# Matmuls that walk their columns from last to first: a two-layer encoder on one core of Trainium2

## The chip, the cores and the metric

The kernel runs on one core of one Trainium2 chip. The time of a run is the device time of that core in microseconds (us). Three runs of the kernel before stand at 1179.58, 1178.33 and 1178.8 us, so the median is 1178.8 us. One further execution was recorded by the hardware profiler; every row of a trace below comes from such a profiled execution.

A core has a matrix unit (TensorE, called PE), which multiplies a stationary tile that it holds by a moving tile that streams through it column by column, and writes the product into a bank of the accumulator memory PSUM. VectorE (DVE), ScalarE (ACT) and GpSimd (POOL) do elementwise work and reductions; SyncE (SP) issues most of the transfers. The loading of a stationary tile is shown on a row of its own, PEld.

## The reference, cut to what matters

The input is x of 512 tokens by 1024 channels in float32. Two layers follow one another. In each, x is normalised, scaled and shifted by a vector from the conditioning c, and projected by `w_in` (1024 by 7328 columns). The projection feeds three attention branches that run over the same 512 tokens: one with low-rank keys and values (MLA, 8 heads), one over a window of three blocks of 128 keys with a sink (SWA, 8 heads), and one that subtracts two softmaxes (differential, 4 heads). Each branch result is gated, projected back and merged:

```python
h = rms_norm(x, g_pre[l]) * (1.0 + scale) + shift
(cq, ckv, kr, za, qb_, kb_, vb_, zb, qc, kc, vc, zc, gcols) = split_cols(h @ w_in[l], IN_SPLITS)
o_a = (mla_branch(...) * jax.nn.silu(za)) @ w_o_mla[l]
o_b = (swa_branch(...) * jax.nn.silu(zb)) @ w_o_swa[l]
o_c = (diff_branch(...) * jax.nn.silu(zc)) @ w_o_diff[l]
g = jax.nn.sigmoid(gcols).reshape(B, S, N_BRANCH, D)
y = (g[:, :, 0] * o_a + g[:, :, 1] * o_b + g[:, :, 2] * o_c) @ w_out[l]
x = x + gate * rms_norm(y, g_post[l])
```

All of it is asked for in float32.

## The kernel before, in words

Almost every product is made of float32 values that are split in two parts, a rounded high part and what is left of it (dtype float32r in the code). A product of two split operands is three matmuls into the same bank: high by high, high by low, low by high. That is `mm3` (lines 86 to 89). It is called for the projections (`proj_T`, `mla_in_step`), the MLA weights, scores and values, the products with the attention weights of the differential branch, the merges (`merge_steps`) and the output projection (`out_phase`). Where one operand carries its two parts stacked in the partitions, two matmuls do: the scores of the SWA branch (lines 878 and 879), those of the differential branch (lines 952 and 953), and `av_step` (lines 713 to 717) for attention weights by values. Sums over the channels that are to be on all partitions are products with a tile of ones (lines 300 and 301 in `gate_rows`, 983 and 984 in `diff_attention`).

The moving tile is float32r, 512 columns wide in nearly all cases, 416 in the first projection of a layer and 256 or 384 in the SWA scores. The matmul's result covers the same number of columns of one bank. All tiles are walked in ascending column order: column 0 of the moving tile goes to column 0 of the bank first.

Other work on PE: transposes against an identity tile (lines 704, 823, 630, 631, 381, 346, 171; moving tile of 128 columns at most), and a few products with one column or in plain float32 (lines 194, 212, 257, 438).

The weights stream from HBM through `wunit`: SP issues a 512 KB load into a `wr` buffer, ACT makes the rounded high part (line 81), DVE subtracts it from the whole (line 84), and PE takes both as stationary tiles. ACT and DVE also empty the eight banks of PSUM: softmax, squares, copies into the split form. A bank is read after the last matmul of its group has ended, and it is used again after its readers have ended.

The order of the work on each engine is set by the framework's planner: `tile.TileContext(nc, schedule_with_timeline_sim=True)` (line 1216) orders instructions by its own estimates of durations and by the priorities that the kernel gives (`tc.high_priority`, `behind`). Dependencies between instructions, and so the semaphores they wait on, follow from the tiles that they read and write.

Of the kernel before, what the change touches and what calls it, by code (L numbers as in the profile page):

```python
# [50 lines left out]
def hybrid_kernel(ctx, tc, x, c, w_ada, b_ada, g_pre, g_post, w_in, g_q, w_uq, g_kv, w_ukv,  # L51
# [6 lines left out]
    pe, act, dve, pool, sp = nc.tensor, nc.scalar, nc.vector, nc.gpsimd, nc.sync  # L58
# [24 lines left out]
    def sub(out_, a, b, eng=None):  # L83
        return (eng or dve).tensor_tensor(out=out_, in0=a, in1=b, op=ALU.subtract)  # L84

    def mm3(o, ah, al, bh, bl, start, stop):
        pe.matmul(o, ah, bh, start=start, stop=False)  # L87
        pe.matmul(o, ah, bl, start=False, stop=False)  # L88
        pe.matmul(o, al, bh, start=False, stop=stop)  # L89

    fence = []

# [39 lines left out]
    onesr = T("onesr", [P, P], F32R)  # L132
# [151 lines left out]
    def gate_rows(l):  # L284
        bg_step(100)
        acc = gate_acc[0]
        gg = []
        for hf in range(2):
            lo = hf * S
            g = T("x5", [P, 896])  # L290
            sp.dma_start(out=g[:, :S], in_=b_ada[l:l + 1, 2 * D + lo:2 * D + lo + S]
                         .broadcast_to([P, S]))
            gp = T("tf", [P, S])
            sp.dma_start(out=gp, in_=g_post[l:l + 1, lo:lo + S].broadcast_to([P, S]))
            pg = Q("sc")
            ah = T("pt", [P, S], F32R)
            al = T("pt", [P, S], F32R)
            act_copy(ah, acc[:, lo:lo + S])
            sub(al, acc[:, lo:lo + S], f(ah))
            pe.matmul(pg, onesr, ah, start=True, stop=False)  # L300
            pe.matmul(pg, onesr, al, start=False, stop=True)
            dve.tensor_tensor(out=g[:, :S], in0=pg, in1=g[:, :S], op=ALU.add)
            dve.tensor_tensor(out=g[:, :S], in0=g[:, :S], in1=gp, op=ALU.mult)
            gg.append(g[:, :S])
        return gg
# [404 lines left out]

    def av_step(av, v, ph, pl, first, last):
        if not last:
            pe.matmul(av, v, ph, start=first, stop=False)  # L713
            pe.matmul(av[0:64], v[:, 0:64], pl, start=False, stop=False)  # L714
        else:
            pe.matmul(av[0:64], v[:, 0:64], pl, start=False, stop=False)
            pe.matmul(av, v, ph, start=False, stop=True)

    def mla_attention(l, cl, kp, v, wts):
        o_all = []  # L720
# [131 lines left out]
    def swa_attention(l, qs, kk, vt):  # L852
        o_all = []
        bt = []

        def first(idx):
            g, n = idx // NT, idx % NT
            kh, kl = kk[g]
            if n == 0:
                bt.clear()  # L860
                for i in range(2):
                    b = T("x5", [P, 896])
                    for h in range(2):
                        sp.dma_start(out=b[:, h * 384:(h + 1) * 384],
                                     in_=skewed(bias_s[4 * g + 2 * i + h], 511, 384))
                    bt.extend([b[:, 0:384], b[:, 384:768]])
                o_all.extend(T("o", [P, S]) for _ in range(2))
            k0, k1 = max(n - 1, 0), min(n + 2, NT)
            j0 = (k0 - n + 1) * P
            w = (k1 - k0) * P  # L870
            mx, sm, nm, sk, rr = (stat(4) for _ in range(5))
            pr = T("p", [P, NT, S])
            for i in range(4):
                q = qs[4 * g + i]
                s = Q("sc")
                ts_ = slice(n * P, (n + 1) * P)
                ks_ = slice(k0 * P, k1 * P)
                pe.matmul(s[:, :w], q[:, ts_], kh[:, ks_], start=True, stop=False)
                pe.matmul(s[:, :w], q[:, ts_], kl[:, ks_], start=False, stop=True)
                dve.tensor_tensor_reduce(  # L880
                    out=pr[:, i, :w], in0=s[:, :w], in1=bt[i][:, j0:j0 + w], scale=1.0,
                    scalar=sinkt[:, l * 8 + 4 * g + i:l * 8 + 4 * g + i + 1],
                    op0=ALU.add, op1=ALU.max, accum_out=mx[:, i:i + 1])
                dve.tensor_scalar(out=nm[:, i:i + 1], in0=mx[:, i:i + 1], scalar1=-1.0,  # L884
                                  scalar2=None, op0=ALU.mult)
                act.activation(out=pr[:, i, :w], in_=pr[:, i, :w], func=AF.Exp,  # L886
                               bias=nm[:, i:i + 1], accum_out=sm[:, i:i + 1])
            dve.tensor_tensor(out=sk, in0=sinkt[:, l * 8 + 4 * g:l * 8 + 4 * g + 4], in1=nm,
                              op=ALU.add)
            act.activation(out=sk, in_=sk, func=AF.Exp)  # L890
            dve.tensor_tensor(out=sk, in0=sk, in1=sm, op=ALU.add)
            dve.reciprocal(out=rr, in_=sk)  # L892
            for i in range(4):
                pool.tensor_scalar(out=pr[:, i, :w], in0=pr[:, i, :w], scalar1=rr[:, i:i + 1],  # L894
                                   scalar2=1.0, op0=ALU.mult, op1=ALU.mult)
            return pr

        def second(idx, pr):
            g, n = idx // NT, idx % NT
            ob = o_all[2 * g:2 * g + 2]  # L900
            k0, k1 = max(n - 1, 0), min(n + 2, NT)
            av = Q("av")
            for kb in range(k0, k1):
                ph, pl = transposed_block([pr[:, i, (kb - k0) * P:(kb - k0 + 1) * P]
                                           for i in range(4)])
                av_step(av, vt[:, kb * 2 + g], ph, pl, kb == k0, kb == k1 - 1)
            ol = T("ta", [P, S])
            act_copy(ol[0:64], av[64:128])
            for i in range(4):
                dve.tensor_tensor(out=ob[i // 2][(i % 2) * 64:(i % 2) * 64 + 64, n * P:(n + 1) * P],  # L910
                                  in0=av[0:64, i * P:(i + 1) * P],
                                  in1=ol[0:64, i * P:(i + 1) * P], op=ALU.add)

        pipelined(first, second, 2 * NT)
        return o_all

# [20 lines left out]
    def diff_attention(l, hh, hl, fill):  # L937
# [3 lines left out]
        def first(hd):  # L941
            qq, kh, kl, vt = ops[hd]
            b = T("x5", [P, 896])
            sp.dma_start(out=b, in_=skewed(bias_d[hd], 1023, 896))
            pr = T("p", [P, NT, S])
            for t in range(NT):
                ts_ = slice(t * P, (t + 1) * P)
                mx, nm, sm, rr = (stat(2) for _ in range(4))
                pc = [pr[:, t], T("ta", [P, S])]
                for i in range(2):  # L950
                    s = Q("sc")
                    pe.matmul(s, qq[i][:, ts_], kh[i], start=True, stop=False)  # L952
                    pe.matmul(s, qq[i][:, ts_], kl[i], start=False, stop=True)  # L953
                    dve.tensor_tensor_reduce(out=pc[i], in0=s, in1=b[:, 384 - t * P:896 - t * P],
                                             scale=1.0, scalar=-3.0e38, op0=ALU.add, op1=ALU.max,
                                             accum_out=mx[:, i:i + 1])
                    dve.tensor_scalar(out=nm[:, i:i + 1], in0=mx[:, i:i + 1], scalar1=-1.0,  # L957
                                      scalar2=None, op0=ALU.mult)
                    act.activation(out=pc[i], in_=pc[i], func=AF.Exp, bias=nm[:, i:i + 1],  # L959
                                   accum_out=sm[:, i:i + 1])  # L960
                dve.reciprocal(out=rr, in_=sm)
                dve.tensor_tensor(out=rr[:, 1:2], in0=rr[:, 1:2], in1=lam_neg[l], op=ALU.mult)
                pool.tensor_scalar(out=pc[1], in0=pc[1], scalar1=rr[:, 1:2], scalar2=1.0,  # L963
                                   op0=ALU.mult, op1=ALU.mult)
                dve.scalar_tensor_tensor(out=pc[0], in0=pc[0], scalar=rr[:, 0:1], in1=pc[1],
                                         op0=ALU.mult, op1=ALU.add)
            return pr

        def second(hd, pr):
            vt = ops[hd][3]  # L970
            av = Q("av")
            for kb in range(NT):
                ph, pl = transposed_block([pr[:, t, kb * P:(kb + 1) * P] for t in range(NT)])
# [3 lines left out]
            sqh = T("pt", [P, S], F32R)  # L977
            sql = T("pt", [P, S], F32R)
# [1 line left out]
            act_copy(sqh, sq)  # L980
            sub(sql, sq, f(sqh))
            sq_ps = Q("pj")
            pe.matmul(sq_ps, onesr, sqh, start=True, stop=False)
            pe.matmul(sq_ps, onesr, sql, start=False, stop=True)
            rs = T("ta", [P, S])
            act.activation(out=rs, in_=sq_ps, func=AF.Ln, scale=1.0 / P, bias=epsc)
            act.activation(out=rs, in_=rs, func=AF.Exp, scale=-0.5)
            o = T("o", [P, S])
# [231 lines left out]
```

## Time and profile before

| what | number |
|---|---|
| median of 3 runs | 1178.8 us (1178.33 to 1179.58) |
| the profiled execution's own time | 1178.78 us |
| its span, first to last instruction | 1176.7 us |
| what lies around the span | 2.1 us |
| PE busy, matmuls | 1146.0 us (97%), 5428 matmuls |
| DVE busy | 844.2 us (72%) |
| ACT busy | 631.5 us (54%) |
| mean granted TensorE clock | 0.993 of full speed |

A matmul's busy time in these tables runs from its start to its modelled end and overlaps the next one's, so it isn't what a matmul costs in a dense stream. That cost is the distance between the starts of two matmuls that follow each other without a wait, which is read from the timeline. "PEclk" or "granted clock" is the share of full speed that the clock gate let through. In a row by groups the columns are line, engine, operation, output and inputs (the moving tile first), shapes, count, then busy time, mean ns of one, and the idle time before them with what ended it.

### The profile page before, as it was taken

What the parts mean: (1) busy time and instruction counts of PE and PEld (TensorE: products, weight loads), DVE (VectorE), ACT (ScalarE), POOL (GpSimd) and SP (SyncE); (2) the same over time, 40 slices, a digit from 0 to 9 for tenths busy, and PEclk for the clock granted to TensorE, in tenths of its full rate; (3) what the DMA queues carried; (4) which work ended last, traced back from release to release, by engine and by line L of the source; (5) the groups of instructions that cost most, each with busy time, mean ns of one, the idle gap of its engine ahead of it and who ended that gap; (6) DMA issues with size and microseconds to landing.
All of it is one profiled execution on the core that took longest, in us unless ns stands there. A gap on an engine that the chain in (4) does not pass through costs nothing.

```text
span 1176.7 us, 15536 instructions
## 1 busy us (share of the span) xinstructions
PE 1146.0 (97%) x5428; PEld 946.0 (80%) x5428; DVE 844.2 (72%) x1754; ACT 631.5 (54%) x1250; POOL 181.3 (15%) x226
## 2 busy tenths in 40 slices
PE   5899999999999999999999999999999999999997
PEld 4768788878887888888888888888888888888886
DVE  7956686898866687876577567688786568786654
ACT  5355464655543457664357456565564346675432
POOL 4310212122210010101211011222121001100120
PEclk9899999999999999999999999999999999999999
DMA  9537532256355433433454432324533333334442
GB/s 340 190 92 217 186 106 76 72 145 186 108 141 164 110 81 87 117 107 126 143 184 135 114 108 75 86 52 123 157 97 92 95 95 96 88 99 115 136 159 92
DMA packets 169522, 146.86 MB, mean 125 GB/s; under 512 B 7679, under 2 KB 146999, under 8 KB 169444
## 3 DMA queue, kind: packets, MB, share of 16 engines
q1 hardware_dynamic: 166148, 140.08, 40.9%
q10 hardware_dynamic: 3168, 5.77, 1.3%
q8 instruction: 43, 0.70, 0.2%
q14 instruction: 35, 0.29, 0.1%
q0 software_dynamic: 128, 0.01, 0.0%
HBM read 135.83 MB, written 14.20 MB: 127 GB/s over the span
## 4 chain that ended last, share of the span: by engine, by line
PE 84%; DVE 6%; DMA 3%; issue 3%; ACT 1%; POOL 1%; SPq 0%; DVEq 0%; POOLq 0%; ACTq 0%
PE ps_dn L87 20%; PE ps_dn L89 20%; PE ps_dn L88 19%; PE ps_tr L704 5%; PE ps_sc L89 2%; PE ps_sc L87 2%; PE ps_sc L88 2%; PE ps_av L714 1%; PE ps_av L713 1%; PE ps_sc L952 1%; PE ps_sc L953 1%; DMA wr<-in_w_in 1%; DVE o L206 1%; PE ps_pj L87 1%; PE ps_pj L88 1%
## 5 line engine op out<-in xcount | busy, mean ns | idle before, releaser
L87 PE MATMUL ps_dn<-hTh,wh 128*128 128x512 f32 x840 | 331.8, 395 | 1.4 <-DVE zz L479 0.8
L89 PE MATMUL ps_dn<-hTh,wl 128*128 128x512 f32 x840 | 330.5, 393 | 0.4 <-DVE wl L84 0.4
L88 PE MATMUL ps_dn<-hTl,wh 128*128 128x512 f32 x840 | 330.1, 393 | 0.0
L84 DVE TENSOR_TENSOR wl<-wr,wh 128x1024 fp32r<-128x1024 f32 x141 | 178.9, 1269 | 98.5 <-ACT wh L81 97.5
L81 ACT ACTIVATE wh<-wr 128x1024 fp32r<-128x1024 f32 x141 | 149.1, 1058 | 162.7 <-PE ps_dn L88 111.2
L87 PEld LDWEIGHTS ps_dn<-hTh,wh 128*128 128x128 f32 x840 | 158.2, 188 | 33.2 <-PE ps_dn L89 1.0
L89 PEld LDWEIGHTS ps_dn<-hTh,wl 128*128 128x128 f32 x840 | 158.0, 188 | 33.3 <-DVE wl L84 0.9
L88 PEld LDWEIGHTS ps_dn<-hTl,wh 128*128 128x128 f32 x840 | 158.1, 188 | 31.7
L84 DVE TENSOR_TENSOR pt<-ps_tr,pt 128x512 fp32r<-128x512 f32 x136 | 92.2, 684 | 30.5 <-ACT pt L81 29.6
L81 ACT ACTIVATE pt<-ps_tr 128x512 fp32r<-128x512 f32 x136 | 78.8, 596 | 64.8 <-PE ps_tr L704 63.6
L775 POOL TENSOR_SCALAR p<-p,st 128x512 f32<-128x512 f32 x64 | 52.2, 834 | 279.3 <-DVE st L773 243.7
L704 PE MATMUL ps_tr<-ident,p 128*128 128x128 f32 x544 | 92.4, 273 | 0.9 <-POOL p L775 0.6
L704 PEld LDWEIGHTS ps_tr<-ident,p 128*128 128x128 f32 x544 | 69.5, 141 | 20.2 <-POOL p L775 1.8
L87 PE MATMUL ps_dn<-u,wh 128*128 128x512 f32 x192 | 75.9, 395 | 0.0
L89 PE MATMUL ps_dn<-u,wl 128*128 128x512 f32 x192 | 75.9, 395 | 0.0
L88 PE MATMUL ps_dn<-u,wh 128*128 128x512 f32 x192 | 75.2, 391 | 0.0
L963 POOL TENSOR_SCALAR ta<-ta,st 128x512 f32<-128x512 f32 x32 | 26.7, 834 | 306.9 <-ACT wh L81 143.1
L894 POOL TENSOR_SCALAR p<-p,st 128x256 f32<-128x256 f32 (+1 forms) x64 | 42.1, 676 | 157.7 <-DVE st L892 130.4
L771 ACT ACTIVATE p<-ps_sc,st 128x512 f32<-128x512 f32 x64 | 43.7, 685 | 28.0 <-DVE st L770 27.7
L770 DVE TENSOR_REDUCE st<-ps_sc 128x1 f32<-128x512 f32 x64 | 43.4, 686 | 21.3 <-PE ps_sc L89 20.8
L886 ACT ACTIVATE p<-p,st 128x256 f32<-128x256 f32 (+1 forms) x64 | 35.7, 558 | 21.9 <-DVE st L884 21.2
L959 ACT ACTIVATE p<-p,st 128x512 f32<-128x512 f32 x32 | 23.1, 723 | 38.8 <-DVE st L957 38.7
(345 smaller groups left out, 2100.5 us busy)
## 6 DMA issues: line engine op xcount, KB each, us to landing
wr<-in_w_in SPq DMA_DIRECT2D x105, 512.0 KB, 3.7
wr<-in_w_ada SPq DMA_DIRECT2D x32, 512.0 KB, 3.6
wr<-in_w_out SPq DMA_DIRECT2D x16, 512.0 KB, 3.6
big<-in_w_ada SPq DMA_DIRECT2D x10, 512.0 KB, 7.6
big<-in_x SPq DMA_DIRECT2D x8, 512.0 KB, 5.3
wr<-in_w_o_mla SPq DMA_DIRECT2D x8, 512.0 KB, 4.0
wr<-in_w_o_swa SPq DMA_DIRECT2D x8, 512.0 KB, 3.4
wr<-in_w_o_diff SPq DMA_DIRECT2D x8, 512.0 KB, 3.7
```

The costliest lines, as they stand in the source:

```text
L81: return act.activation(out=out_, in_=in_, func=AF.Copy, scale=scale)
L84: return (eng or dve).tensor_tensor(out=out_, in0=a, in1=b, op=ALU.subtract)
L87: pe.matmul(o, ah, bh, start=start, stop=False)
L88: pe.matmul(o, ah, bl, start=False, stop=False)
L89: pe.matmul(o, al, bh, start=False, stop=stop)
L704: pe.transpose(tr[:, i * P:(i + 1) * P], b, ident)
L770: dve.tensor_reduce(out=nm[:, t:t + 1], in_=s, axis=AX.X, op=ALU.max, negate=True)
L771: act.activation(out=pr[:, t], in_=s, func=AF.Exp, bias=nm[:, t:t + 1], accum_out=sm[:, t:t + 1])
L775: pool.tensor_scalar(out=pr[:, t], in0=pr[:, t], scalar1=rr[:, t:t + 1], scalar2=1.0, op0=ALU.mult, op1=ALU.mult)
L886: act.activation(out=pr[:, i, :w], in_=pr[:, i, :w], func=AF.Exp, bias=nm[:, i:i + 1], accum_out=sm[:, i:i + 1])
L894: pool.tensor_scalar(out=pr[:, i, :w], in0=pr[:, i, :w], scalar1=rr[:, i:i + 1], scalar2=1.0, op0=ALU.mult, op1=ALU.mult)
L963: pool.tensor_scalar(out=pc[1], in0=pc[1], scalar1=rr[:, 1:2], scalar2=1.0, op0=ALU.mult, op1=ALU.mult)
```

## The change

A new helper, `rmm`, gives a matmul its output and its moving tile through views with the column axis reversed. The stationary tile is passed as it was. The last column of the moving tile is then read first, and its product is written to the last column of the bank first; each column of the bank still receives the product of the same column of the moving tile. `mm3` calls `rmm` three times, and the pairs of matmuls in `gate_rows`, `av_step`, `swa_attention` and `diff_attention` call it too. The transposes, the matmuls of lines 194, 212, 257 and 438, and all work on the other engines are as before.

```diff
+    def rmm(o, a, b, start, stop):
+        pe.matmul(o[:, ::-1], a, b[:, ::-1], start=start, stop=stop)
+
     def mm3(o, ah, al, bh, bl, start, stop):
-        pe.matmul(o, ah, bh, start=start, stop=False)
-        pe.matmul(o, ah, bl, start=False, stop=False)
-        pe.matmul(o, al, bh, start=False, stop=stop)
+        rmm(o, ah, bh, start, False)
+        rmm(o, ah, bl, False, False)
+        rmm(o, al, bh, False, stop)
...
-            pe.matmul(pg, onesr, ah, start=True, stop=False)
-            pe.matmul(pg, onesr, al, start=False, stop=True)
+            rmm(pg, onesr, ah, start=True, stop=False)
+            rmm(pg, onesr, al, start=False, stop=True)
...
     def av_step(av, v, ph, pl, first, last):
         if not last:
-            pe.matmul(av, v, ph, start=first, stop=False)
-            pe.matmul(av[0:64], v[:, 0:64], pl, start=False, stop=False)
+            rmm(av, v, ph, start=first, stop=False)
+            rmm(av[0:64], v[:, 0:64], pl, start=False, stop=False)
         else:
-            pe.matmul(av[0:64], v[:, 0:64], pl, start=False, stop=False)
-            pe.matmul(av, v, ph, start=False, stop=True)
+            rmm(av[0:64], v[:, 0:64], pl, start=False, stop=False)
+            rmm(av, v, ph, start=False, stop=True)
...
-                pe.matmul(s[:, :w], q[:, ts_], kh[:, ks_], start=True, stop=False)
-                pe.matmul(s[:, :w], q[:, ts_], kl[:, ks_], start=False, stop=True)
+                rmm(s[:, :w], q[:, ts_], kh[:, ks_], start=True, stop=False)
+                rmm(s[:, :w], q[:, ts_], kl[:, ks_], start=False, stop=True)
...
-                    pe.matmul(s, qq[i][:, ts_], kh[i], start=True, stop=False)
-                    pe.matmul(s, qq[i][:, ts_], kl[i], start=False, stop=True)
+                    rmm(s, qq[i][:, ts_], kh[i], start=True, stop=False)
+                    rmm(s, qq[i][:, ts_], kl[i], start=False, stop=True)
...
-            pe.matmul(sq_ps, onesr, sqh, start=True, stop=False)
-            pe.matmul(sq_ps, onesr, sql, start=False, stop=True)
+            rmm(sq_ps, onesr, sqh, start=True, stop=False)
+            rmm(sq_ps, onesr, sql, start=False, stop=True)
```

## The prediction, made before the changed kernel was built or run

> **What bounds the kernel now.** I read the page's busy table and clock line first, then the chain that ended last, then busy time by stretches, and last the timeline of PE. The first fence is from the page: the span, two engine rows, the granted clock in 40 slices, and the chain by engine and by line.
>
> ```profile
> span 1176.7 us, 15536 instructions
> PE 1146.0 (97%) x5428; PEld 946.0 (80%) x5428; DVE 844.2 (72%) x1754; ACT 631.5 (54%) x1250; POOL 181.3 (15%) x226
> ...
> PEclk9899999999999999999999999999999999999999
> ...
> PE 84%; DVE 6%; DMA 3%; issue 3%; ACT 1%; POOL 1%; SPq 0%; DVEq 0%; POOLq 0%; ACTq 0%
> PE ps_dn L87 20%; PE ps_dn L89 20%; PE ps_dn L88 19%; PE ps_tr L704 5%; PE ps_sc L89 2%; PE ps_sc L87 2%; PE ps_sc L88 2%; PE ps_av L714 1%; PE ps_av L713 1%; PE ps_sc L952 1%; PE ps_sc L953 1%; DMA wr<-in_w_in 1%; DVE o L206 1%; PE ps_pj L87 1%; PE ps_pj L88 1%
> ```
>
> The reader is to see that the chain is PE for 84% of the span, and within it the three lines of `mm3`. The next fence splits the span in three; its columns are the stretch, its length, then busy time and count of PE, PEld, DVE, ACT and POOL, the granted clock, the share of DMA and GB/s.
>
> ```profile
> 0.00:60.00 60.00, 41.10 (x196) 35.98 (x197) 49.40 (x122) 28.61 (x55) 24.21 (x29) 0.91 0.77 262
> 60.00:1150.00 1090.00, 1084.22 (x5144) 893.22 (x5143) 782.31 (x1608) 598.14 (x1181) 154.86 (x194) 1.00 0.41 118
> 1150.00:1176.70 26.70, 20.66 (x92) 16.77 (x90) 12.45 (x25) 4.71 (x16) 2.21 (x4) 0.96 0.21 79
> ```
>
> Between 60 and 1150 us PE lacks 1090.00 - 1084.22 = 5.8 us of being busy throughout, at full clock. So in 93% of the span a matmul that took longer would lengthen the kernel by just that much, and one that took less would shorten it, until DVE (782.31 us busy there) became the bound. Nothing covers a change in the cost of a matmul.
>
> What a matmul costs stands in the timeline: start in us, busy us, then the instruction. The first pair of rows is the first and the last of 15 matmuls of 512 columns in an unbroken stream; the second pair, the first and the last of four of 256 columns, with the transpose that follows them.
>
> ```profile
> 599.82 0.39 PE L87 MATMUL ps_dn<-big,op 128*128 128x512 f32 x1
> ...
> 602.99 0.40 PE L89 MATMUL ps_dn<-wh,pt 128*128 128x512 f32 x1
> ...
> 299.88 0.28 PE L878 MATMUL ps_sc<-op,op 128*128 128x256 f32 x1
> ...
> 300.23 0.28 PE L879 MATMUL ps_sc<-op,op 128*128 128x256 f32 x1
> 300.35 0.27 PE L704 MATMUL ps_tr<-ident,p 128*128 128x128 f32 x1
> ```
>
> From 599.82 to 602.99 are 14 distances, so 3.17 / 14 = 0.2264 us for 512 columns; from 299.88 to 300.35 are 4, so 0.118 us for 256. The difference is 0.109 us for 256 columns, 0.42 ns a column. The cost of a matmul is thus mainly its columns, with some 0.01 us that don't depend on them.
>
> **The change part by part.** Nothing is removed, added or moved among the instructions. Each call of `rmm` issues the one matmul that stood there, with the same stationary tile, the same number of columns, the same bank and the same flags. No transfer, no wait and no queue is touched, so nothing new stands behind a waiting instruction. What changes is the direction in which 4,664 matmuls step through the moving tile in SBUF and through the bank in PSUM. The count: the next fence has `mm3`'s three lines (stretches of the whole span restricted to lines 87, 88 and 89, in this order), and the groups of the paired matmuls.
>
> ```profile
> 0.00:1176.70 1176.70, 544.59 (x1392) 263.37 (x1392) 0.99 0.42 125
> ...
> 0.00:1176.70 1176.70, 544.67 (x1392) 262.85 (x1392) 0.99 0.42 125
> ...
> 0.00:1176.70 1176.70, 539.42 (x1392) 262.43 (x1392) 0.99 0.42 125
> ...
> L713 PE MATMUL ps_av<-pt,big 128*128 128x512 f32 x72 | 29.2, 406 | 0.9 <-DVE st L884 0.9
> ...
> L952 PE MATMUL ps_sc<-op,op 128*128 128x512 f32 x64 | 25.4, 407 | 0.0
> ...
> L717 PE MATMUL ps_av<-pt,big 128*128 128x512 f32 x32 | 12.6, 393 | 0.0
> ...
> L878 PE MATMUL ps_sc<-op,op 128*128 128x384 f32 x32 | 11.5, 360 | 0.0
> ...
> L878 PE MATMUL ps_sc<-op,op 128*128 128x256 f32 x32 | 8.9, 293 | 1.1 <-DVE st L880 1.1
> ...
> L983 PE MATMUL ps_pj<-pt,onesr 128*128 128x512 f32 x8 | 3.5, 434 | 0.0
> ...
> L300 PE MATMUL ps_sc<-pt,onesr 128*128 128x512 f32 x4 | 1.6, 389 | 0.0
> ```
>
> Three times 1,392 is 4,176. Each of the seven other groups has a partner of the same count in the line beside it (two matmuls a pair): 2 x (72 + 64 + 32 + 32 + 32 + 8 + 4) = 488. Together 4,664 of PE's 5,428; the other 764 are the transposes and small products. In columns: 64 matmuls have 384, 64 have 256, and 192 of `mm3`'s have 416 (8 channel blocks x 4 token blocks x 3 matmuls x 2 layers, from `mla_in_step`); the other 4,344 have 512. That makes 2,344,960 columns, as many as 4,580 matmuls of 512 have.
>
> No row of this trace shows an operand of a matmul that is stepped through backwards, so the price of a column in that order is bounded from both sides. *From below:* a column can't go through faster than the clock, so at most the part that isn't columns could shrink. That part follows from a stretch where the clock was halved. The first row of the next fence is that stretch (its eighth number is the granted clock, 0.50); the other two are the first and the last of four matmuls of 512 columns in it.
>
> ```profile
> 36.00:37.50 1.50, 1.50 (x5) 1.13 (x4) 1.50 (x7) 1.00 (x2) 0.00 (x0) 0.50 0.92 280
> ...
> 36.08 0.63 PE L87 MATMUL ps_dn<-hTh,pt 128*128 128x512 f32 x1
> ...
> 37.36 0.63 PE L88 MATMUL ps_tr<-hTl,pt 128*128 128x512 f32 x1
> ```
>
> 1.28 us / 3 = 0.4267 us for 512 columns at half clock. If that is columns alone, they take 0.2133 us at full clock, and 0.2264 - 0.2133 = 0.013 us a matmul is the rest. If all of it went, 4,664 x 0.013 = 61 us would be gained: 1118 us is the floor. *From above:* the nearest row in which columns pass more slowly is the same one, at one column in two full-clock periods, 0.4267 us for 512, worked out below as a rival.
>
> Between these ends I take zero, an unchanged 0.2264 us. The row it leans on is the stream itself: each column is four bytes next to the one before it, in the moving tile and in the bank, and this neighbourhood is the same in either direction. All groups have even widths, so two neighbours that are fetched or written together going up are also together going down. A group of accumulating matmuls is reversed as a whole; column n of one matmul meets column n of the next 0.2264 us later, as before. Loading the stationary tile isn't touched, and its cover stays: a load takes 188 ns against 226 ns from matmul to matmul (first row below).
>
> ```profile
> L87 PEld LDWEIGHTS ps_dn<-hTh,wh 128*128 128x128 f32 x840 | 158.2, 188 | 33.2 <-PE ps_dn L89 1.0 <-DVE zz L479 1.0
> ...
> 307.55 0.48 PE L87 MATMUL ps_dn<-hTh,wh 128*128 128x512 f32 x1
> 307.87 0.39 PE L88 MATMUL ps_dn<-hTl,wh 128*128 128x512 f32 x1
> ```
>
> The sum: the profiled execution's span of 1176.7 us, plus 4,664 x 0, plus the 2.1 us around it, is 1178.8 us. The median of the three runs is 1178.8 too, so nothing has to be moved between them. For scale: 0.2% of the time, about what a measurement of this kernel can tell from no change, is 2.4 us, or 0.5 ns a matmul. A very small cost would be seen.
>
> **The rivals.**
>
> *Half rate (slower).* The full rate needs two neighbouring columns taken in one access, and the logic that pairs them only knows the upward step; going down, each column is an access of its own. The place is every one of the 4,664 matmuls, and it decides from the first, as nothing covers them. Price: 0.4267 - 0.2264 = 0.200 us for 512 columns by the half-clock row; 4,580 x 0.200 = 917 us, so 2096 us. If the 0.013 us stays on top, 4,580 x 0.213 = 977 us, so 2156 us. For it: 0.2133 of 0.2264 us are columns at the full clock, so a slower access has no slack to hide in, and the trace has no stepped operand that shows one. Against it: pairs stay neighbours in reverse.
>
> The Trainium skill speaks for this rival: "Advanced Engine Details and Errata", section "PSUM Cachelines", and "PSUM — Partial Sum Buffer", section "Specifications (TRN2)", say that PSUM has 8-byte lines and that any non-contiguous pattern slows matmuls significantly. By a strict reading a step of -1 is such a pattern, and the sum would be that of this rival. The first page adds that every two consecutive elements should be contiguous, which a backward walk over even widths fulfils; by that reading the sum is mine. No run so far shows either.
>
> *A small price for each matmul (slower).* The direction costs a turn at the start of each matmul, not a rate: the walk begins at the far end. Bounds: above zero, up to what a restart costs in this trace. The two rows just shown, right after a transpose, lie 0.32 us apart in place of 0.2264, so 0.09 us; for all 4,664 that is 420 us. A doubling of the 0.013 us is nearer to what is in question and gives 1178.8 + 61 = 1240 us. Against it: no first column of a stream has such a turn today.
>
> *Another order (either sign).* The planner orders the instructions by its own estimates. If it prices a reversed operand otherwise, the same instructions come in another order, and PE's few waits move. What can be lost or won is of the size of the gaps: 5.8 us between 60 and 1150 us, and those of the first 60 us, of which these are PE's waits on other engines:
>
> ```profile
> PE ps_sc L346 <- DVE st L318: 4.1, 1, 4.1
> PE ps_sc L87 <- ACT hTh L81: 2.9, 1, 2.9
> PE ps_tr L212 <- DVE o L206: 2.4, 1, 2.4
> ```
>
> So 1173 to 1185 us. For it: the priorities lie close together. Against it: shapes and types are the same.
>
> *A gain.* Some of the 0.013 us between matmuls goes: 1118 us at most, 1160 us for a third of it. I see nothing in the profile for it.
>
> *The change doesn't do what it says.* Both views are reversed, so the builder could turn both back and emit the old instructions. The time would be 1178.8 us, as in the forecast.
>
> **How the numbers follow.** The forecast of no change gets 0.50, and the builder that turns it back 0.02 with the same time. Half rate gets 0.24, because its only witness against is symmetry; the small price 0.10; another order 0.10, of which 0.04 faster, 0.02 within and 0.04 slower; a gain 0.04. So faster by over 0.2% is 0.08, within 0.2% is 0.54, slower is 0.38. The predicted time is the likeliest's, 1178.8 us; its own range is 1176 to 1182 us. That holds little over half, and with the small price still under 0.8, so the range has to reach into half rate, whose two ends are 2096 and 2156: it goes up to 2160 us. Downward it takes in the planner's gain and the smallest part of the other: 1170 us.
>
> **What would show it.** Right: the dense stream still has 0.226 us from start to start for 512 columns, `mm3`'s lines have 1,392 matmuls each with the same mean, 15,536 instructions, and the span is 1176.7 us. Half rate: the distance becomes 0.43 us at a granted clock of 1.00 while transposes keep theirs; the small price: 256 and 512 columns grow by the same ns; another order: distances unchanged, but the waits of PE and the sequence of lines differ. Wrong is the forecast if the distance for 512 columns moves by more than 0.5 ns, whichever way.

## The result: 1.6% slower, and the profile after

The changed kernel took 1197.91 us (median of 4 runs, 1197.23 to 1199.2) against 1179.19 us for the kernel before. The ratio is 1.0161, with a 95% interval of 1.0143 to 1.0178. The forecast was no change. The profiled execution of the changed kernel took 1197.91 us with a span of 1196.0 us.

The page of the changed kernel, the lines that answer to those shown of before. All reversed matmuls now stand on line 87, the line of `rmm`:

```profile
span 1196.0 us, 15542 instructions
PE 1168.5 (98%) x5428; PEld 947.7 (79%) x5428; DVE 846.4 (71%) x1754; ACT 631.8 (53%) x1250; POOL 180.4 (15%) x226
...
PEclk9899999999999999999999999999999999999999
...
PE 88%; DVE 5%; DMA 3%; issue 1%; ACT 1%; POOL 1%; SPq 0%; DVEq 0%; POOLq 0%; ACTq 0%
...
L87 PE MATMUL ps_dn<-hTh,wh 128*128 128x512 f32 x840 | 337.5, 402 | 0.2
```

The counts are the same, 5,428 matmuls; so is the granted clock. The mean of one projection matmul went from 395 to 402 ns, and PE has a larger share of the chain. The stretches of the changed kernel, in the columns used before, with the middle one ending where as much is left as in the kernel before (26.7 us):

```profile
0.00:60.00 60.00, 41.10 (x189) 35.80 (x190) 49.27 (x122) 28.90 (x55) 24.43 (x29) 0.89 0.77 262
...
60.00:1169.30 1109.30, 1106.71 (x5154) 895.60 (x5153) 785.28 (x1608) 598.75 (x1183) 153.74 (x194) 1.00 0.40 116
1169.30:1196.00 26.70, 20.65 (x89) 16.31 (x87) 11.84 (x25) 4.12 (x14) 2.21 (x4) 0.96 0.21 79
```

With both ends cut at the same length, the loss falls on the middle: 1109.30 us in place of 1090.00, with nearly the same work on the other engines. It holds 5,154 matmuls in place of 5,144; the ten more are some 2 us of it (an estimate at 0.23 us each). PE lacks 2.6 us of being busy throughout there, and lacked 5.8 before; it isn't waiting, it is slower. The timeline of PE in a dense stream, first and last of 11 matmuls:

```profile
615.02 0.40 PE L87 MATMUL ps_dn<-wh,op 128*128 128x512 f32 x1
...
617.35 0.40 PE L87 MATMUL ps_dn<-wl,op 128*128 128x512 f32 x1
```

2.33 us over 10 distances are 0.233 us, where the kernel before had 0.2264. PE executes the same instructions in the same order in both kernels, so the distance from each matmul's start to the next one's can be compared pair by pair. Worked out from the starts of all 5,428:

```text
512 columns, by distance before   count   mean before   mean after   sum of differences
up to 229 ns                       3255     226.7 ns      233.4 ns       +21.7 us
230 to 249 ns                       851     232.9         233.7           +0.7
250 to 340 ns                       211     314.5         317.1           +0.6
over 340 ns (waits)                  26     610.4         508.2           -2.7
all other matmuls                  1084                                   -0.8
```

So 3,255 matmuls went from 226.7 to 233.4 ns, which is 6.7 ns. The 851 that were at 230 to 249 ns already paid nearly nothing: 233 ns is a level that is reached, not an amount that is added.

At half clock there is no price at all. The changed kernel has a stretch like the one that the prediction used (its eighth number is the granted clock); the other rows are the first and the last of four reversed matmuls of 512 columns in it:

```profile
35.40:37.20 1.80, 1.80 (x6) 1.36 (x5) 1.80 (x8) 0.92 (x2) 0.00 (x0) 0.50 0.95 299
...
35.45 0.63 PE L87 MATMUL ps_dn<-hTl,pt 128*128 128x512 f32 x1
...
36.73 0.63 PE L87 MATMUL ps_tr<-hTh,pt 128*128 128x512 f32 x1
```

1.28 us / 3 = 0.4267 us, exactly what the ascending ones took in the kernel before. Of the eleven reversed distances of 512 columns at half clock ten are 426 or 427 ns; the eleventh, at the start of a stream, is 572, as its like in the kernel before is. The 416-column ones take 346 or 347 ns there, so 96 columns are 80 ns, 512 are 427, and nothing is left over. So neither the 6.7 ns nor the 13 ns that the prediction called the rest is an amount on top of the columns: both show only at the full clock. That would fit something that goes on beside the columns and is the longer of the two at full clock, but this is argued, not shown.

### The profile page after: what moved, and what is told of

The parts are those of the page before. It is cut to its first block, busy times and chain, and to the rows that moved or that the text cites. A ratio compares the mean times of both kernels' runs of the same rounds, so it can differ in the third digit from the quotient of the medians.

```text
span 1196.0 us, 15542 instructions
## 1 busy us (share of the span) xinstructions
PE 1168.5 (98%) x5428; PEld 947.7 (79%) x5428; DVE 846.4 (71%) x1754; ACT 631.8 (53%) x1250; POOL 180.4 (15%) x226
## 4 chain that ended last, share of the span: by engine, by line
PE 88%; DVE 5%; DMA 3%; issue 1%; ACT 1%; POOL 1%; SPq 0%; DVEq 0%; POOLq 0%; ACTq 0%
PE ps_dn L87 60%; PE ps_sc L87 11%; PE ps_av L87 7%; PE ps_tr L707 5%; PE ps_pj L87 4%; DVE o L209 2%; DMA wr<-in_w_ada 1%; DMA wr<-in_w_in 1%; DVE wl L84 1%; DVE u L254 1%; DVE hTl L84 0%; DMA rk<-in_rope_k 0%; PE ps_pj L826 0%; POOL p L778 0%; DMA tf<-in_g_pre 0%
## 5 line engine op out<-in xcount | busy, mean ns | idle before, releaser
L87 PE MATMUL ps_dn<-hTh,wh 128*128 128x512 f32 x840 | 337.5, 402 | 0.2
L87 PE MATMUL ps_dn<-hTh,wl 128*128 128x512 f32 x840 | 336.3, 400 | 0.2 <-DVE wl L84 0.2
L87 PE MATMUL ps_dn<-hTl,wh 128*128 128x512 f32 x840 | 336.1, 400 | 0.0
L87 PE MATMUL ps_sc<-op,op 128*128 128x512 f32 (+2 forms) x448 | 126.8, 383 | 0.8 <-DVE st L883 0.8
L87 PE MATMUL ps_dn<-u,wh 128*128 128x512 f32 x384 | 124.4, 400 | 0.0
L87 PE MATMUL ps_av<-pt,big 128*128 128x512 f32 (+1 forms) x304 | 100.6, 406 | 0.9 <-DVE st L887 0.9
L87 PEld LDWEIGHTS ps_sc<-op,op 128*128 128x128 f32 x448 | 79.5, 189 | 16.6 <-DVE st L883 1.0
L87 PEld LDWEIGHTS ps_dn<-u,wh 128*128 128x128 f32 x384 | 71.5, 188 | 16.4
L966 POOL TENSOR_SCALAR ta<-ta,st 128x512 f32<-128x512 f32 x32 | 26.7, 836 | 314.1 <-DVE st L965 132.5
L87 PEld LDWEIGHTS ps_av<-pt,big 128*128 128x128 f32 (+1 forms) x304 | 50.7, 170 | 14.7 <-DVE st L887 1.2
```

Source lines behind the costliest of these rows:

```text
L87: pe.matmul(o[:, ::-1], a, b[:, ::-1], start=start, stop=stop)
```

## The experiments

**Reading alone, and writing alone.** The reversal has two halves. Each was taken back by itself.

```diff
-        pe.matmul(o[:, ::-1], a, b[:, ::-1], start=start, stop=stop)
+        pe.matmul(o, a, b[:, ::-1], start=start, stop=stop)        # reading alone
+        pe.matmul(o[:, ::-1], a, b, start=start, stop=stop)        # writing alone
```

> Only the moving tile is read from last to first; the bank is written ascending, so the columns of every product come out mirrored, and the output is not the reference's. Instructions, order and waits are those of the changed kernel. Theory R (the price of 5.4 ns per 512-column matmul lies in reading the moving tile downward): the dense stream goes at 233 ns as after, and the time is about 1198 us (ratio to before 1.016). Theory W (it lies in writing the bank downward): 227 ns and 1179 us (ratio 1.000). Theory B (either direction has a part): in between, 1185 to 1193 us.

> Only the bank is written from last to first; the moving tile is read ascending, so the columns come out mirrored, and the output is not the reference's. Theory R: 227 ns from start to start and 1179 us. Theory W: 233 ns and 1198 us. Theory B: in between, and the two prices of the two runs add up to about 19 us.

Reading alone: 1198.96 us, ratio 1.0156 (1.0140 to 1.0171). Writing alone: 1180.19 us, ratio 1.0000 (0.9989 to 1.0012). The timeline of PE, reading alone (first and last of 12), then writing alone (first and last of 9):

```profile
599.09 0.40 PE L87 MATMUL ps_dn<-wh,op 128*128 128x512 f32 x1
...
601.65 0.40 PE L87 MATMUL ps_dn<-wh,pt 128*128 128x512 f32 x1
```

```profile
596.75 0.39 PE L87 MATMUL ps_dn<-wh,op 128*128 128x512 f32 x1
...
598.56 0.39 PE L87 MATMUL ps_dn<-wh,pt 128*128 128x512 f32 x1
```

2.56 us over 11 distances are 0.233 us; 1.81 over 8 are 0.226. Theory R holds: the whole price lies in reading the moving tile downward. Writing a bank from its last column to its first costs nothing that these runs can tell. The strict reading of the Trainium skill's "PSUM — Partial Sum Buffer", section "Specifications (TRN2)", that any non-contiguous pattern slows matmuls significantly, does not extend to a step of -1 in the bank.

**Streams without the encoder.** Does the price go by the matmul, by the column, or by the pair of neighbours?

```diff
+    for k in range(N):
+        pe.matmul(banks[1], st(k), mv(k), **fl(k))
+    for k in range(N):
+        pe.matmul(banks[2][:, ::-1], st(k), mv(k)[:, ::-1], **fl(k))
...
+    for k in range(N):
+        pe.matmul(banks[7], st(k), mv(k)[:, ::-1] if k % 2 else mv(k), **fl(k))
```

> Not the encoder: streams of 40 accumulating matmuls, one line of the kernel for each stream, with nothing else at work at first; the output is not the reference's. Ascending 512 columns: 226.7 ns from start to start; both reversed: 233.3 ns. Reading alone and writing alone reversed: theory R 233.3 and 226.7, theory W the other way round. If the price is a turn for each matmul, 496, 416, 384, 320 and 256 columns pay the same 6.7 ns; if it goes with the columns, 416 pay 5.4, 384 pay 5.0 and 256 pay 3.3. Alternating directions: the mean of both, 230 ns, if each matmul pays for itself; 226.7 or 233.3 if it goes by the pair. Blocks of 16 columns taken downward with ascending columns inside: 226.7 if single steps cost, 233.3 if the far end as starting point costs. Tile shifted by 2 or 14 columns: same prices if alignment plays no part. With loads under way, the ascending stream should show some distances of 231 to 236 as the kernel before does, and the reversed one should stay at 233.

The timeline of PE; each row is one stream, with its start, so the start of the next row less its own, over its count, is the distance. In order: 512 columns ascending, both reversed, reading alone, writing alone; then ascending and reversed at 416, 384, 320, 256 and 496; then alternating directions; then ascending from 2 columns later.

```profile
17.92 9.23 PE L46 MATMUL ps_b<-m,w 128*128 128x512 f32 x40
26.99 9.50 PE L48 MATMUL ps_b<-m,w 128*128 128x512 f32 x40
36.33 9.50 PE L50 MATMUL ps_b<-m,w 128*128 128x512 f32 x40
45.66 9.25 PE L52 MATMUL ps_b<-m,w 128*128 128x512 f32 x40
54.74 7.63 PE L54 MATMUL ps_b<-m,w 128*128 128x416 f32 x40
62.21 7.80 PE L56 MATMUL ps_b<-m,w 128*128 128x416 f32 x40
69.85 7.10 PE L58 MATMUL ps_b<-m,w 128*128 128x384 f32 x40
76.79 7.27 PE L60 MATMUL ps_b<-m,w 128*128 128x384 f32 x40
83.89 6.03 PE L62 MATMUL ps_b<-m,w 128*128 128x320 f32 x40
89.76 6.03 PE L64 MATMUL ps_b<-m,w 128*128 128x320 f32 x40
95.62 4.96 PE L66 MATMUL ps_b<-m,w 128*128 128x256 f32 x40
100.42 4.90 PE L68 MATMUL ps_b<-m,w 128*128 128x256 f32 x40
105.16 8.97 PE L70 MATMUL ps_b<-m,w 128*128 128x496 f32 x40
113.97 9.23 PE L72 MATMUL ps_b<-m,w 128*128 128x496 f32 x40
123.03 9.36 PE L74 MATMUL ps_b<-m,w 128*128 128x512 f32 x40
132.23 9.51 PE L76 MATMUL ps_b<-m,w 128*128 128x512 f32 x40
141.58 9.59 PE L78 MATMUL ps_b<-m,w 128*128 128x512 f32 x40
```

From L46 on the distances are 0.227, 0.2335, 0.233 and 0.227 us: reading costs, writing doesn't, with nothing else at work. At 416 columns it is 0.187 against 0.191, at 384 0.1735 against 0.1775, at 320 0.147 against 0.1465, at 256 0.120 against 0.1185, at 496 0.220 against 0.2265. The price is neither a fixed turn nor a rate. It is about 6.6 ns at 512 and 496, about 4 ns at 416 and 384, and none at 320 and 256 (the ascending stream of 416 was at 0.188 in the next run, which leaves 3 ns there). Alternating directions give 0.230, the mean, so each matmul pays for itself.

Blocks of 16 columns taken downward with ascending columns inside them went at 0.233 us, so single downward steps aren't needed for the price. Two things were not foreseen. Ascending blocks with descending columns inside went at 0.2665 us. And the ascending tile that begins 2 columns later (L76) went at 0.234 us, as slowly as a reversed one. In this run the loads meant to run beside the last streams had all landed by then, so it says nothing on loads at work there. They ran during the first two streams of 512 shown above, at some 290 GB/s by the page, and these still kept 0.227 and 0.2335 us.

**Where the tile begins, and other engines at work.** If an ascending tile can be slow by its place, is the reversed one slow only because it begins at an odd place, its column 511?

```diff
+    for k in range(N):
+        pe.matmul(banks[3], st(k), mv(k, S, 2), **fl(k))
...
+    for k in range(N):
+        pe.matmul(banks[6][:, ::-1], st(k), mv(k, S, 1)[:, ::-1], **fl(k))
```

> Not the encoder: streams of 24 accumulating matmuls, each line of the kernel with another first column of the moving tile, ascending or both views reversed; the last four streams have VectorE or ScalarE at work beside them; the output is not the reference's. The streams before showed that an ascending tile that begins 2 columns later goes at 233.8 ns and one that begins 14 later at 230, against 226.7. Theory S (the price goes with the place of the first column that is read, not with the direction): the ascending distance depends on the shift with a period of 4, 8 or 16 columns and is 226.7 again at 16; a reversed tile that starts on the right column (shifted by 1, from column 512 on) goes at 226.7. Theory D (reading downward costs by itself): no shift of the reversed tile comes below 233. Widths 416 and 384 reversed and shifted by 1: theory S gives back 186.7 and 173.3, theory D keeps 191 and 178. Beside VectorE or ScalarE: if their traffic makes the distances of 231 to 236 in the kernel before, the ascending stream shows such distances and the reversed one stays at 233.3.

Ascending, shifts of 1, 2, 3, 4, 6, 8, 10, 12, 14, 15 and 16 columns gave distances of 236.7, 233.3, 228.9, 231.7, 233.3, 233.4, 233.4, 233.4, 230.0, 226.8 and 228.8 ns, against 226.7 unshifted (means without the first few matmuls of a stream, which differ). No period of 4, 8 or 16. Reversed, no shift came below 233.3 ns; shifted by 1, so that it begins at column 512, it was 235.6, and by 3, the slowest, 239.8. At 416 and 384 columns the reversed streams took 191.0 and 177.7 ns unshifted, 193.4 and 177.9 shifted by 1, 189.0 and 179.7 shifted by 8. Of this run's timeline, the reversed stream without a shift, the ones shifted by 1 and 2, and the row that follows; then, with VectorE beside them, an ascending and a reversed stream, and the row after:

```profile
81.51 5.77 PE L71 MATMUL ps_b<-m,w 128*128 128x512 f32 x24
87.11 5.82 PE L73 MATMUL ps_b<-m,w 128*128 128x512 f32 x24
92.77 5.84 PE L75 MATMUL ps_b<-m,w 128*128 128x512 f32 x24
98.45 5.92 PE L77 MATMUL ps_b<-m,w 128*128 128x512 f32 x24
...
195.94 11.09 PE L125 MATMUL ps_b<-m,w 128*128 128x512 f32 x48
206.87 11.37 PE L130 MATMUL ps_b<-m,w 128*128 128x512 f32 x48
218.07 11.06 PE L135 MATMUL ps_b<-m,w 128*128 128x512 f32 x48
```

Theory S falls, theory D holds in this: at 512 columns a downward walk stays at 233 ns or more wherever it begins, and at 416 and 384 it doesn't go back to the 186.7 and 173.3 ns that theory S gave.

The ascending stream beside VectorE has a mean of 0.228 us, but not because of VectorE. Its slow distances are the first ten, 224 to 236 ns; the next thirty, still beside the additions (the last ends at 205.1 us), are 226 or 227. The one beside ScalarE's copies begins with 238 and 232 ns and keeps 226 or 227 from the third on. What these streams show is that a stream takes some matmuls to settle behind another one. The kernel before shows the same. Take the matmuls of 512 columns with a stationary tile of 128, in the order in which they follow one another without a different matmul or a gap (250 ns or more) between them. Of the first ten in such a row, 741 of 1,426 took 230 ns or more; of the later ones, 39 of 2,598. Of the later ones with VectorE busy for over 95% of the distance it was 14 of 1,393, of those with under 5% 14 of 764. So most of the 851 slow ones stood near the start of a row, and nothing here puts them down to VectorE. Why a row settles so is open.

**The stationary tile.** The next stationary tile is loaded while the moving tile streams: PEld is busy for 947.7 us beside PE's 1168.5. Do the two reads clash?

```diff
+    for k in range(N):
+        pe.matmul(banks[1][0:16], st(k, 16), mv(k), **fl(k))
+    for k in range(N):
+        pe.matmul(banks[2][0:16][:, ::-1], st(k, 16), mv(k)[:, ::-1], **fl(k))
```

> Not the encoder: streams of 24 accumulating matmuls of 512 columns in pairs, ascending and then both views reversed, with stationary tiles of 128, 96, 64, 32 and 16 columns, stationary tiles that begin 1 to 64 columns later, one stationary tile for all, one moving tile for all, and both operands out of one tile; the output is not the reference's. Theory L (the price is a clash of the downward walk with the loading of the next stationary tile, which goes on meanwhile): price falls with the columns of the stationary tile, about 3.3 ns at 64 and 1 ns or nothing at 16, and the distance of the ascending stream falls too; it changes with the start of the stationary tile. Theory M (it lies in the walk over the moving tile alone): 6.7 ns at every size of the stationary tile and at every start of it.

Its timeline, the pair at 128 columns of stationary tile and the next row, then the pair at 16 and the next row:

```profile
14.25 5.60 PE L47 MATMUL ps_b<-m,w 128*128 128x512 f32 x24
19.69 5.77 PE L49 MATMUL ps_b<-m,w 128*128 128x512 f32 x24
25.30 5.69 PE L51 MATMUL ps_b<-m,w 128*96 128x512 f32 x24
...
58.70 5.72 PE L63 MATMUL ps_b<-m,w 128*16 128x512 f32 x24
64.26 5.76 PE L65 MATMUL ps_b<-m,w 128*16 128x512 f32 x24
69.86 5.74 PE L67 MATMUL ps_b<-m,w 128*128 128x512 f32 x24
```

The reversed streams are at 0.233 us with 128 and with 16 columns. Theory L, with a price that falls with the load, is out. But theory M isn't right either: the ascending stream got slower with the smaller tile, 0.230 us at 96 and 64 columns and 0.232 at 32 and 16, and it took 230.7 to 233.5 ns with a stationary tile that begins 1 to 32 columns later (227.8 at 64). One stationary or one moving tile for all changed nothing. So the ascending 226.7 ns is the special case: in these runs it needs the place of both operands to be right, and all 128 columns of the stationary tile. The reversed stream stays between 233 and 237 ns throughout.

**Only the projections reversed.**

```diff
     def rmm(o, a, b, start, stop):
-        pe.matmul(o[:, ::-1], a, b[:, ::-1], start=start, stop=stop)
+        pe.matmul(o, a, b, start=start, stop=stop)
...
+    def mm3r(o, ah, al, bh, bl, start, stop):
+        mm3(o[:, ::-1], ah, al, bh[:, ::-1], bl[:, ::-1], start, stop)
...
-            mm3(acc, wh[:, k * P:(k + 1) * P], wl[:, k * P:(k + 1) * P], hh[:, k], hl[:, k],
+            mm3r(acc, wh[:, k * P:(k + 1) * P], wl[:, k * P:(k + 1) * P], hh[:, k], hl[:, k],
```

> Only proj_T has both views reversed (2,496 of the 4,664 matmuls, moving tile hT); all others ascend. If each matmul pays for itself: 2,496 x 5.4 ns = 13.5 us of longer distances, of which the same share is won back in waits as in the changed kernel (19.3 of 22.4 us arrive), so 11 to 12 us, 1190 to 1191 us, ratio 1.010. If the price were made by a part that isn't counted in matmuls (another order, the ends of groups), no such proportion.

1193.64 us, ratio 1.0116 (1.0099 to 1.0133), 2 to 3 us more than expected. Of the 512-column distances that were up to 229 ns before, the 1,963 of reversed matmuls grew by 6.8 ns each, 13.3 us, as expected. The 1,292 of ascending ones grew too, by 2.6 us in all, and 15.2 us arrived in the span (1191.9 us). Of the 2.6 us, 1.8 lie in the first two ascending matmuls behind a reversed one: the first took 236.5 ns (138 of them), the second 231.5 (101), where they took 226.8 in the kernel before. The streams show the same turn: the stream of writing alone, which reads upward and follows one that reads downward, begins with 238 and 232 ns and then stays at 226 or 227. Why the alternating stream, at 227 and 233 ns, doesn't pay for its turns is open.

**An ascending kernel on other addresses.** If the start of an ascending tile prices it, the kernel before should become slower by a shift alone.

```diff
+SH = 2
...
-        return T("hTh", [P, KT, S], F32R), T("hTl", [P, KT, S], F32R)
+        return [T(n, [P, KT * S + 16], F32R)[:, SH:SH + KT * S]
+                .rearrange("p (k s) -> p k s", k=KT) for n in ("hTh", "hTl")]
```

> No view is reversed; the tiles hTh and hTl begin 2 columns (8 bytes) later in their buffer, so that every projection reads its moving tile ascending from there. If the starting place prices an ascending matmul in this kernel as it did in the streams (233.3 in place of 226.7 ns), some 2,500 matmuls pay up to 6.7 ns: 1189 to 1194 us, without any reversal. If the place of the first column plays no part in the kernel: 1179 us.

1196.45 us, ratio 1.0148 (1.0130 to 1.0166): more than expected. The two buffers had grown by 64 bytes. In the kernel before, the moving and the stationary tile of all 4,344 float32r matmuls of 512 columns begin on multiples of 512 bytes, by the addresses of the built program. Now 1,224 of the 1,752 matmuls whose moving tile isn't hT had it 128 bytes off, and 896 of all 4,344 their stationary tile. The matmuls with other moving tiles that were up to 229 ns went from 226.7 to 232.5 ns. So the run was repeated with 512 bytes more in place of 64 (`KT * S + 128`), once with the shift of 2 columns and once with one of 128.

> No view is reversed; hTh and hTl begin 2 columns later in a buffer that is 128 columns longer, so that all other tiles stay on multiples of 512 bytes, which they didn't in the run before. If the first column's place is what an ascending matmul pays for: the moving hT's matmuls (2,544) at 232 to 233 ns in place of 228, the others unchanged, 1189 to 1193 us. If the earlier run's loss came from the other tiles: 1179 to 1182 us.

> As the run beside it, but hTh and hTl begin 128 columns (512 bytes) later, on such a multiple again: 1179 us if the place within 512 bytes decides; 1189 to 1193 us if any other place than the buffer's start costs.

Shift of 2 columns: 1191.96 us, ratio 1.0106 (1.0089 to 1.0123). Shift of 128: 1179.58 us, ratio 1.0000 (0.9991 to 1.0009). Groups of the run with a shift of 2 columns, a moving tile that is shifted and one that isn't; then the same two with a shift of 128:

```profile
L88 PE MATMUL ps_dn<-hTh,wh 128*128 128x512 f32 x840 | 336.5, 401 | 0.3 <-DVE op L809 0.2
...
L88 PE MATMUL ps_dn<-u,wh 128*128 128x512 f32 x192 | 76.1, 396 | 0.0
```

```profile
L88 PE MATMUL ps_dn<-hTh,wh 128*128 128x512 f32 x840 | 332.0, 395 | 0.7 <-DVE op L809 0.5 <-DVE zz L481 0.2
...
L88 PE MATMUL ps_dn<-u,wh 128*128 128x512 f32 x192 | 75.9, 395 | 0.0
```

In the first run the shifted tile has 401 ns and the other 396; with a shift of 128 columns both have 395, as before. Eight bytes of shift cost the kernel 1.06%, without any reversal.

**More widths, 64 rows, and two-byte elements.**

```diff
+    for k in range(N):
+        pe.matmul(banks[5], sb16(k), mv16(k), **fl(k))
+    for k in range(N):
+        pe.matmul(banks[6][:, ::-1], sb16(k), mv16(k)[:, ::-1], **fl(k))
```

> Not the encoder: more pairs of streams of 24 matmuls, ascending and then reversed: 288, 352, 448 and 480 columns; 512 columns from a tile that begins 32, 64, 96 or 128 columns later; 64 rows in place of 128; and bfloat16 tiles of 512, 384 and 256 columns; the output is not the reference's. If the reversed walk adds a fixed stall once a matmul is long enough, 352 to 448 columns pay 4.4 ns and 480 pays 6.7, as 384, 416, 496 and 512 did, and 288 pays nothing. If the price comes from four-byte elements passing more slowly downward, bfloat16 pays less or nothing. Ascending from 128 columns later (512 bytes) should be back at 226.7; from 32, 64 or 96 in between.

In pairs, ascending and reversed: 131.7 and 133.1 ns at 288 columns, 161.2 and 162.3 at 352, 202.7 and 206.7 at 448, 216.7 and 220.0 at 480; 228.3 and 233.3 with 64 rows (226 or 227 once the ascending one has settled). Ascending from 64 and from 128 columns later 227.2, from 32 and 96 later 232.4, so what counts is the place within 256 bytes. The timeline, the ascending streams from 32 and 64 columns later with the reversed one after each, then bfloat16 ascending and reversed and the row after:

```profile
60.61 5.74 PE L77 MATMUL ps_b<-m,w 128*128 128x512 f32 x24
66.19 5.84 PE L79 MATMUL ps_b<-m,w 128*128 128x512 f32 x24
71.87 5.63 PE L81 MATMUL ps_b<-m,w 128*128 128x512 f32 x24
77.33 5.77 PE L83 MATMUL ps_b<-m,w 128*128 128x512 f32 x24
...
116.64 5.35 PE L97 MATMUL ps_b<-mb,wb 128*128 128x512 bf16 x24
121.83 5.34 PE L99 MATMUL ps_b<-mb,wb 128*128 128x512 bf16 x24
127.01 4.06 PE L101 MATMUL ps_b<-mb,wb 128*128 128x384 bf16 x24
```

The bfloat16 streams are at 0.216 us in both directions: no price, and none at 384 (162.5 ns) and 256 columns (109.2) either. That agrees with the 215.7 ns that the Trainium skill gives for 512 columns back to back ("TensorE: Matmul & The Clock Gate", section "Wait — 56ns, not 53.3ns?"). The float32r streams have some 11 ns more even in the best case.

## Why the prediction was wrong, point by point

- **What bounds the kernel.** Right. PE sets the end, nothing covers a matmul that gets slower, and 19.3 of the 20.3 us by which the 512-column distances grew arrived in the span.
- **The counts.** Right: 4,664 matmuls, no other instruction on the engines' rows. That no wait is touched was wrong, but without a price: see "another order".
- **The price of a column in reverse.** This is the step that failed: "Between these ends I take zero". The term 4,664 x 0 should have been 6.7 ns each for those 512-column matmuls that stand in a dense stream at the best distance, 3,255 of them, 21.7 us. The reason given, that neighbours stay neighbours, holds for the bank, where the runs show nothing. It doesn't hold for the moving tile. There it took symmetry between two directions for granted, and the 226.7 ns of the trace were in truth a best case that holds for an upward walk from a favourable place.
- **The bounds.** They held, 1118 to 2156 us, but the lower price lay in the 0.013 us "that isn't columns", which I had only looked at as something that could shrink: at full clock it grew to 0.020. It was also misread as a fixed part of each matmul, for at half clock nothing of it is left, in either direction.
- **Half rate.** Wrong. The distance grew by 3%, not 89%, at the same granted clock.
- **A small price for each matmul.** Nearest: slower, by the matmul, not covered. Its size was taken as a doubling of the 0.013 us (61 us); half of it came, on part of the matmuls. Its mechanism, a turn at the start, isn't what the widths show (none at 320 columns, 4 ns at 384, 6.7 at 512), and a turn of fixed length would stand at half clock too, where there is none.
- **Another order.** Wrong. Compared line by line, the built programs have the same order on all five engines. Both the changed kernel and writing alone have other waits on some matmuls and 6 instructions more (15,542), and writing alone costs nothing; reading alone has 15,536, and costs all.
- **A gain, and a change that doesn't do what it says.** Wrong: the distance moved, upward.

What stays open is why a float32r matmul of 512 columns that reads downward takes 233.3 ns at full clock and not 226.7. It isn't the bank, the columns of the stationary tile, the rows, the loads or the order. There is no price with two-byte elements, none at half clock, and at most 1.5 ns from 352 columns down. An upward walk from an unfavourable place costs as much, so it is likely one cause with two triggers, but that is argued, not shown; the place counts for a reversed tile too, which took 239.8 ns shifted by 3 columns, where the ascending one took 228.9.

## What to carry to other kernels

Where a stream of float32r matmuls sets the time, the distance from start to start is worth checking against the best one: here 226.7 ns for 512 columns, and it was lost by reversing the moving tile or by moving it 8 bytes off its multiple of 256 bytes. A pad that is added to one buffer can cost the tiles behind it (here 232.5 ns for 226.7); after such an edit compare the distance in a dense stream, past its first ten matmuls, and not the busy time. And an operand's direction or place that no row of the trace shows has no price of zero by symmetry: it needs a small stream of its own, which tells it in one run.

## What the runs showed of the hardware that was not expected

- The direction in which a bank is written is free (ratio 1.0000), the direction in which the moving tile is read isn't (1.0156).
- The place of the moving tile and of the stationary tile within 256 bytes moves an ascending float32r matmul of 512 columns between 226.7 and 236.7 ns. The kernel before has all of them on multiples of 512 bytes.
- At half clock the two directions cost the same, 426 or 427 ns for 512 columns.
- An ascending stream needs up to ten matmuls to settle at 226.7 ns behind other work on PE; a reversed one is at 233 or 234 ns nearly from its start. VectorE at work beside it changed neither.
- Descending columns inside ascending blocks of 16 are the worst pattern tried, 266.7 ns.
